# Transposing gated blocks by DMA: the steps of a block set one or more steps apart

## The chip, the cores and the metric

The kernel runs on one core of one Trainium2 chip. A core has five engines that run their own instruction streams and meet through semaphores: PE (TensorE, matrix products), DVE (VectorE), ACT (ScalarE), POOL (GpSimd) and SP (SyncE, which here only issues DMAs). The metric is the device time of one execution in microseconds (us), the median of several runs. Lower is better.

## The reference

One decoder layer for 256 tokens of width 2048, in float32: half an FFN, a parallel mixer of sliding-window attention and an RWKV-7 recurrence, cross-attention into a memory, half an FFN, and a last norm. The change lies in the two FFNs (inner width 5632):

```python
def swiglu(h, w_gate, w_up, w_down):
    return (jax.nn.silu(h @ w_gate) * (h @ w_up)) @ w_down
...
        x = x + 0.5 * swiglu(rms_norm(x, ffn1_norm[l]), ffn1_w_gate[l], ffn1_w_up[l], ffn1_w_down[l])
        x = gated_parallel_mixer(x, mix_norm[l], ...)
        x = memory_cross_attention(x, mem, cross_norm[l], ...)
        x = x + 0.5 * swiglu(rms_norm(x, ffn2_norm[l]), ffn2_w_gate[l], ffn2_w_up[l], ffn2_w_down[l])
    return rms_norm(x, final_norm)
```

## The kernel before

**Products.** A float32 factor is split into a high part, rounded to the type that TensorE multiplies (fp32r), and the rest. A product is then three: high by high, rest by high, high by rest (`times`, L449, L450, L451). Weights stream from HBM in pieces of 1 MB (`raw`, L326). ACT casts the high part `hi` (L372), DVE subtracts for the rest `lo` (L373). PE's matmuls add up in PSUM banks named `acc`, `mm` and `tr`.

**Gate and up together.** `gate_and_up` works out a block of 512 inner columns of both weights through `product_pair`: eight steps q over the width of 2048, two chunks of 128 rows each. Some steps (q = 0, 2, 4 in the first FFN, 0, 2, 3, 4 in the second) are done as seven products instead of eight, by a scheme like Strassen's: DVE forms four combinations of the gate and up weights (L401 to L404), ACT casts them (`thi`, L380), DVE subtracts (`tlo`, L381). For q = 3 the combinations were staged in DRAM (`sums`) and are loaded from there. After the last of the seven-product steps ACT copies a PSUM bank into the new block `hb` (L593), and DVE adds up the results (L596 to L608) into the gated block: `hb`, 256 tokens by 512 columns, as [128, 2, 512].

**Turning a block.** The down product needs the gated block with its columns on the partitions. An FFN has 11 blocks in three groups of 4, 4 and 3. The last block of each group is transposed by TensorE, the other eight, sixteen in both FFNs, by DMA: the generator `turned`. Its transposes work on 16-bit elements, so a float32 block goes as two halves. ACT copies the low and the high halves of all words apart (two `uh`, L761), four DMA transposes on SP's queue bring them into `ht` (L767; the first two carry the one half, the other two the other half), four ACT copies join the halves to float32 words again (two for each of two tiles `u`, L772: the first needs transposes one and two, the second three and four), and each `u` is split (`hhi` by ACT, L649, `hlo` by DVE, L650).

**What sets the order.** `turned` runs in the background of the next block's `gate_and_up`: `Interleave.tick` resumes each running generator up to its next `yield`, and `product_pair` ticks three times in a seven-product step, four times in another one. So a `yield` is one step, a dozen matmuls or less. Where the last seven-product step ends, `first` runs all steps that are still left (`until`), since it needs the tiles. From the start of `gate_and_up` to there are 15 ticks in the first FFN, 14 in the second. Each engine works through its own instructions in the order that results, ACT's and SP's included; the tile scheduler may move PE's.

Blocks are numbered 0 to 15 here, in the order in which they are turned: 0 to 7 in the first FFN, 8 to 15 in the second. Block 7 is turned from 618 us on, block 12 from 1876 us on.

Of the kernel before, what the change touches and what calls it, by code (L numbers as in the profile page):

```python
# [137 lines left out]
def decoder_layer(ctx: ExitStack, tc: tile.TileContext, a: dict, out: bass.AP):  # L138
    nc = tc.nc
    act, dve, pool, pe = nc.scalar, nc.vector, nc.gpsimd, nc.tensor  # L140
# [18 lines left out]
    def f32(x):  # L159
        return x.bitcast(F32)  # L160
# [14 lines left out]
    def idle(n):  # L175
        for _ in range(n):
            yield
# [94 lines left out]
    for entry in weight_plan(a):  # L272
# [10 lines left out]
        for k in range(k0, k0 + nk, 2 * KU):  # L283
            u = len(units)
# [294 lines left out]
    def sums_of(sp):  # L579
        return (sp.tile([P, 512], F32, tag="u", name="u", bufs=2) for _ in range(2))  # L580
# [56 lines left out]
    def feat(tok, cols):  # L637


        b = tr()  # L640
        for i, col in enumerate(cols):
            for t in range(2):
                o = (2 * i + t) * P
                pe.transpose(b[:, o : o + P], tok[:, t, col : col + P], ident[:])  # L644
        return b[:].rearrange("p (c t) -> p c t", c=2)

    def split(x: Act, c, n, src):

        act.copy(x.at(0, c, n), src)  # L649
        dve.tensor_tensor(x.at(1, c, n), src, f32(x.at(0, c, n)), ALU.subtract)  # L650
        x.done |= set(range(c, c + n))
# [81 lines left out]
    def feed_forward(sp, x, norm: Norm, wg, wu, wd, done, begin_last=lambda: None, last=False):  # L733
        if last:
            for tag, shape, dt, bufs in (
                ("hhi", [P, 16, T], F32R, 1), ("hlo", [P, 16, T], F32R, 1),
                ("hb", [P, 2, 512], F32, 2), ("thia", [P, KU, 512], F32R, 1),
                ("tloa", [P, KU, 512], F32R, 1), ("thib", [P, KU, 512], F32R, 1),
                ("tlob", [P, KU, 512], F32R, 1),
            ):  # L740
                sp.tile(shape, dt, tag=tag, name=tag, bufs=bufs)
        begun = at["item"]
        c = combinations(
            sp, norm.x, SEVEN_2 if last else SEVEN, "c",
            lambda: at["item"] > begun + (4 if last else 7) and not (last and norm.r is None),
        )
        c["next"] = []
        for gi, (j0, nj) in enumerate(GROUPS):
            h = Act(
                [sp.tile([P, 16, T], F32R, tag="hhi", name="hhi")],  # L750
                [sp.tile([P, 16, T], F32R, tag="hlo", name="hlo")], 16,
            )
            ch = combinations(sp, h, SEVEN_DOWN[nj < 4], "d", early=False, n=12)

            def turned(hb, c):

                both = hb[:].rearrange("p t n -> p (t n)")
                src = both.bitcast(U16).rearrange("p (t n e) -> p e t n", t=2, e=2)
                us = [sp.tile([P, 2, 512], U16, tag="u", name="uh", bufs=2) for _ in range(2)]
                for e, u in enumerate(us):  # L760
                    act.copy(u[:], src[:, e])  # L761
                    yield
                dst = sp.tile([P, 2, 2, 4, P], U16, tag="hb", name="ht", bufs=2)
                yield
                for e, u in enumerate(us):
                    for t in range(2):
                        nc.sync.dma_start(dst[:, e, t], u[:, t], transpose=True)  # L767
                yield from idle(7)
                for q, u in enumerate(sums_of(sp)):
                    v = u[:].bitcast(U16).rearrange("p (c t k e) -> p e t c k", c=2, t=2, e=2)  # L770
                    for e in range(2):
                        act.copy(v[:, e], dst[:, e, :, 2 * q : 2 * q + 2, :])  # L772
                    split(h, c + 2 * q, 2, u[:].rearrange("p (c t) -> p c t", c=2))
                    yield

            def transposed(hb, c):
                banks = [feat(hb, [2 * q * P, (2 * q + 1) * P]) for q in range(2)]
                for q, b in enumerate(banks):
                    split(h, c + 2 * q, 2, b)
                    yield  # L780

            for j in range(j0, j0 + nj):
                if j > 0:
                    hb = gate_and_up(sp, norm.x, c, norm.r, wg)

                    turn = transposed if j == j0 + nj - 1 else turned
                    c["next"].append(turn(hb, 4 * (j - j0)))
                    continue
                pg = product(norm.x, wg)
                hb = sp.tile([P, 2, 512], F32, tag="hb", name="hb", bufs=2)  # L790
                if last:
                    for t in range(2):
                        act.activation(hb[:, t, :], pg[t][:], AF.Silu, scale=norm.r[t])
                pu = product(norm.x, wu, bank=acc if last else mm)
                bg.until(lambda: norm.r is not None)
                for t in range(2):
                    if not last:
                        act.activation(hb[:, t, :], pg[t][:], AF.Silu, scale=norm.r[t])
                    dve.scalar_tensor_tensor(
                        hb[:, t, :], pu[t][:], norm.r[t], hb[:, t, :], ALU.mult, ALU.mult  # L800
                    )
                c["next"].append(turned(hb, 0))
            end = gi == len(GROUPS) - 1
            bg.spawn("feat", c["next"].pop())
            if end:
                begin_last()

            def col(t, n):
                return x[:, t, n * 512 : (n + 1) * 512]

            for n in (0, 2):
                if last and end and n:

                    whole = [(t, slice(0, 512)) for t in range(2)]
                    parts_ = [(t, slice(c, c + 256)) for t in range(2) for c in (0, 256)]
                    pieces = {2: whole, 3: parts_}
                    for m in (n, n + 1):
                        pd = product(h, wd, skew=m == 3)
                        for t, cs in pieces[m]:
                            dve.scalar_tensor_tensor(  # L820
                                col(t, m)[:, cs], pd[t][:, cs], 0.5, col(t, m)[:, cs],
                                ALU.mult, ALU.add,
                            )
                            done(m, t, cs)
                    continue
                down(h, ch, wd, [[col(t, n + i) for i in range(2)] for t in range(2)])
                if end:
                    done(n)
                    done(n + 1)
# [1018 lines left out]
```

## Time and profile before

| | |
|---|---|
| median of 3 runs | 2250.27 us (2247.72 to 2253.74) |
| the profiled execution | 2251.8 us |
| its span, first to last instruction | 2250.1 us |
| mean granted clock of TensorE | 0.998 |
| PE busy | 2205.8 us, 98% of the span |
| DVE busy | 1800.1 us, 80% |
| ACT busy | 1341.4 us, 60% |
| DMA transposes | 64, median 5.0 us from issue to landing |

Durations in the trace are of one instruction on its engine; a bracket such as [4.50 <-DMA ht<-uh] tells how long the engine had been idle before it and what ended that. Matmuls overlap: in a row without waits they start 0.23 us apart, and are shown 0.39 us long. SPq is the DMA-issuing work of SP. A line of the view by stages has the stage's bounds, its length, and for each engine the busy time with the number of instructions in brackets.

### The profile page before, as it was taken

To read this page: it belongs to the slowest core of one execution; us is meant where nothing else is said; L and a number is where in the kernel's file an instruction comes from. 1 tells how busy PE (TensorE), PEld (TensorE's weight loads), DVE (VectorE), ACT (ScalarE), POOL (GpSimd) and SP (SyncE) were. 2 spreads that over 40 slices of the span, in tenths; PEclk is the share of its full clock that TensorE was granted. 3 is DMA by queue.
4 is the path that set the end of the run, shared out by engine and by line. 5 is a ranking of instruction groups with operands and counts; after the bars stand their busy time and mean duration, and the time that the engine had idled before them with its cause. 6 is when DMAs were issued, how large, how long until landed. Compare 5 with 4: busy or idle time off the path is not lost.

```text
span 2250.1 us, 28118 instructions
## 1 busy us (share of the span) xinstructions
PE 2205.8 (98%) x10392; PEld 1803.5 (80%) x10392; DVE 1800.1 (80%) x2316; ACT 1341.4 (60%) x1773; POOL 107.0 (5%) x184
## 2 busy tenths in 40 slices
PE   9999999999999999999999999999999999999998
PEld 7778877788878877888888888888768877788776
DVE  7888888898989476877667666458898898998896
ACT  6665556664666577644544546466665566655664
POOL 0000000000000001000331030000000000000000
PEclk9999999999999999999999999999999999999999
DMA  8665666656575645677778787557766666666673
GB/s 301 188 214 187 205 199 213 197 192 220 196 196 194 190 127 161 206 233 213 227 219 282 217 282 252 185 169 274 219 204 217 209 211 213 221 208 204 204 248 135
DMA packets 233097, 474.41 MB, mean 211 GB/s; under 512 B 50336, under 2 KB 52736, under 8 KB 221952
## 3 DMA queue, kind: packets, MB, share of 16 engines
q1 hardware_dynamic: 223792, 446.48, 61.2%
q0 software_dynamic: 7648, 23.52, 3.4%
q10 hardware_dynamic: 1520, 2.63, 0.3%
q8 instruction: 81, 1.33, 0.2%
q14 instruction: 56, 0.46, 0.1%
HBM read 440.49 MB, written 23.59 MB: 206 GB/s over the span
## 4 chain that ended last, share of the span: by engine, by line
PE 76%; DVE 12%; DMA 6%; ACT 2%; issue 2%; SPq 1%; POOLq 0%; POOL 0%; ACTq 0%; DVEq 0%
PE acc L449 17%; PE acc L450 17%; PE acc L451 17%; PE mm L449 5%; PE mm L451 5%; PE mm L450 5%; DVE lo L373 4%; DMA raw<-in_ffn_w_up_dram 3%; DVE tlo L381 2%; DMA ht<-uh 1%; PE tr L644 1%; PE tr L450 1%; PE tr L451 1%; PE tr L449 1%; PE mm L1468 1%
## 5 line engine op out<-in xcount | busy, mean ns | idle before, releaser
L373 DVE TENSOR_TENSOR lo<-raw,hi 128x1024 fp32r<-128x1024 f32 (+1 forms) x768 | 878.3, 1149 | 342.2 <-ACT hi L372 339.7
L372 ACT CAST hi<-raw 128x1024 fp32r<-128x1024 f32 (+1 forms) x768 | 754.4, 992 | 659.4 <-PE acc L451 482.9
L450 PE MATMUL acc<-lo,xhi 128*128 128x512 f32 (+1 forms) x1134 | 441.1, 389 | 8.5 <-DVE lo L373 8.3
L449 PE MATMUL acc<-hi,xhi 128*128 128x512 f32 (+1 forms) x1134 | 444.0, 394 | 5.1 <-ACT hi L372 4.7
L451 PE MATMUL acc<-hi,xlo 128*128 128x512 f32 (+1 forms) x1134 | 439.3, 388 | 0.0
L450 PEld LDWEIGHTS acc<-lo,xhi 128*128 128x128 f32 x1134 | 213.5, 188 | 56.3 <-DVE lo L373 14.9
L449 PEld LDWEIGHTS acc<-hi,xhi 128*128 128x128 f32 x1134 | 213.3, 188 | 53.4 <-ACT hi L372 7.7
L451 PEld LDWEIGHTS acc<-hi,xlo 128*128 128x128 f32 x1134 | 212.9, 188 | 43.1 <-issue 0.4
L381 DVE TENSOR_TENSOR tlo<-raw,thi 128x1024 fp32r<-128x1024 f32 x192 | 232.0, 1219 | 5.2 <-ACT thi L380 4.5
L380 ACT CAST thi<-raw 128x1024 fp32r<-128x1024 f32 x192 | 199.5, 1050 | 49.9 <-DVE raw L403 30.6
L449 PE MATMUL mm<-hi,xhi 128*128 128x512 f32 x402 | 157.3, 392 | 1.5 <-DVE u L598 1.2
L450 PE MATMUL mm<-lo,xhi 128*128 128x512 f32 x402 | 157.0, 391 | 0.0
L451 PE MATMUL mm<-hi,xlo 128*128 128x512 f32 x402 | 156.9, 390 | 0.0
L451 PE MATMUL acc<-hi,hlo 128*128 128x512 f32 x372 | 145.3, 391 | 0.0
L450 PE MATMUL acc<-lo,hhi 128*128 128x512 f32 x372 | 145.3, 391 | 0.0
L449 PE MATMUL acc<-hi,hhi 128*128 128x512 f32 x372 | 145.0, 390 | 0.0
L449 PEld LDWEIGHTS mm<-hi,xhi 128*128 128x128 f32 x402 | 75.7, 188 | 19.7 <-DVE u L598 3.9
L451 PEld LDWEIGHTS mm<-hi,xlo 128*128 128x128 f32 x402 | 75.8, 188 | 16.0
L450 PEld LDWEIGHTS mm<-lo,xhi 128*128 128x128 f32 x402 | 75.7, 188 | 15.6
L450 PEld LDWEIGHTS acc<-lo,hhi 128*128 128x128 f32 x372 | 69.9, 188 | 14.3
L449 PEld LDWEIGHTS acc<-hi,hhi 128*128 128x128 f32 x372 | 69.9, 188 | 14.2
L451 PEld LDWEIGHTS acc<-hi,hlo 128*128 128x128 f32 x372 | 69.9, 188 | 14.1
(445 smaller groups left out, 3583.4 us busy)
## 6 DMA issues: line engine op xcount, KB each, us to landing
raw<-in_ffn_w_down_dram SPq DMA_DIRECT2D x88, 1024.0 KB, 5.2
raw<-in_ffn_w_gate_dram SPq DMA_DIRECT2D x84, 1024.0 KB, 5.3
raw<-in_ffn_w_up_dram SPq DMA_DIRECT2D x78, 1024.0 KB, 6.2
raw<-in_w_in_dram SPq DMA_DIRECT2D x136, 512.0 KB, 3.9
raw<-in_w_out_dram SPq DMA_DIRECT2D x32, 512.0 KB, 4.7
raw<-sums SPq DMA_DIRECT2D x20, 512.0 KB, 6.8
raw<-in_w_proj_attn_dram SPq DMA_DIRECT2D x16, 512.0 KB, 3.9
raw<-in_w_proj_rwkv_dram SPq DMA_DIRECT2D x16, 512.0 KB, 6.4
```

Of the source, the lines that this page charges most:

```text
L372: at["hi"] = act.copy(hi[:, s], raw[:, s])
L373: at["lo"] = dve.tensor_tensor(lo[:, s], raw[:, s], f32(hi[:, s]), ALU.subtract)
L380: act.copy(hi[:], v[:])
L381: dve.tensor_tensor(lo[:], v[:], f32(hi[:]), ALU.subtract)
L449: pe.matmul(o, xh, hi, start=first, stop=False, **how)
L450: pe.matmul(o, xh, lo, start=False, stop=False, **how)
L451: pe.matmul(o, xl, hi, start=False, stop=last, **how)
L644: pe.transpose(b[:, o : o + P], tok[:, t, col : col + P], ident[:])
L1468: pe.matmul(vb[to, (o + k) * P : (o + k + 1) * P][:, r], lhs(k, e), v[:, k, r], start=v is u and k + e == 0, stop=True, **ek,)
```

## The change

Only the generator `turned` is edited. The two copies `uh` come one step later than before and with idle steps between them; every DMA transpose is a step of its own; there are two idle steps before the joins rather than seven; and the joins and the split of each half are two steps.

```diff
--- before.py
+++ after.py
@@ -757,19 +757,21 @@
                 both = hb[:].rearrange("p t n -> p (t n)")
                 src = both.bitcast(U16).rearrange("p (t n e) -> p e t n", t=2, e=2)
                 us = [sp.tile([P, 2, 512], U16, tag="u", name="uh", bufs=2) for _ in range(2)]
-                for e, u in enumerate(us):
-                    act.copy(u[:], src[:, e])
-                    yield
+                yield
+                act.copy(us[0][:], src[:, 0])
+                yield from idle(3)
+                act.copy(us[1][:], src[:, 1])
                 dst = sp.tile([P, 2, 2, 4, P], U16, tag="hb", name="ht", bufs=2)
-                yield
                 for e, u in enumerate(us):
                     for t in range(2):
                         nc.sync.dma_start(dst[:, e, t], u[:, t], transpose=True)
-                yield from idle(7)
+                        yield
+                yield from idle(2)
                 for q, u in enumerate(sums_of(sp)):
                     v = u[:].bitcast(U16).rearrange("p (c t k e) -> p e t c k", c=2, t=2, e=2)
                     for e in range(2):
                         act.copy(v[:, e], dst[:, e, :, 2 * q : 2 * q + 2, :])
+                    yield
                     split(h, c + 2 * q, 2, u[:].rearrange("p (c t) -> p c t", c=2))
                     yield
```

The steps of a block were 13 and are 15. Before: copy; copy; (the tile); four DMAs and seven idle steps; joins and split; joins and split. Now: nothing; copy and three idle; copy, the tile and the first DMA; three DMAs, one a step; two idle; joins; split; joins; split. From the tile on, lines stand two further down (L772 becomes L773), and the second copy is L763. Every engine has the same instructions as before, and as many of them; what changes is where they stand. Three places:

SyncE, block 7. `raw` are the weight loads, `ht<-uh` the transposes. Before:

```order
L326 DMA raw_4918<-in_ffn_w_gate_dram 128x2048
L326 DMA raw_4974<-in_ffn_w_up_dram 128x2048
L767 DMA_TRANSPOSE ht<-uh 128x4x128
L326 DMA raw_5017<-in_ffn_w_gate_dram 128x2048
L767 DMA_TRANSPOSE ht<-uh 128x4x128 x3
L326 DMA raw_5069<-in_ffn_w_up_dram 128x2048
```

Now:

```order
L326 DMA raw_4918<-in_ffn_w_gate_dram 128x2048
L326 DMA raw_4974<-in_ffn_w_up_dram 128x2048
L767 DMA_TRANSPOSE ht<-uh 128x4x128
L326 DMA raw_5015<-in_ffn_w_gate_dram 128x2048
L767 DMA_TRANSPOSE ht<-uh 128x4x128 x2
L326 DMA raw_5068<-in_ffn_w_up_dram 128x2048
L767 DMA_TRANSPOSE ht<-uh 128x4x128
```

The second up load from the top stood behind all four transposes and now stands ahead of the fourth. It is so in each of the sixteen blocks, with gate loads standing between or ahead of the earlier transposes; in blocks 9 and 12 the gate load and the staged sums now also stand ahead of the first.

ACT, block 7, from the cast of the next step's `thi` on; `u<-ht` are the joins. Before:

```order
L380 CAST thi<-raw 128x1024
L372 CAST hi<-raw_4974 128x512
L380 CAST thi<-raw 128x1024
L772 COPY u<-ht 128x2x2x128 x2
L372 CAST hi<-raw_4918 128x1024
L649 CAST hhi<-u 128x512
L772 COPY u<-ht 128x2x2x128 x2
L372 CAST hi<-raw_4974 128x1024
L372 CAST hi<-raw_5017 128x1024
L649 CAST hhi<-u 128x512
L380 CAST thi<-raw 128x1024
L372 CAST hi<-raw_5069 128x512
```

Now:

```order
L380 CAST thi<-raw 128x1024
L372 CAST hi<-raw_4974 128x512
L380 CAST thi<-raw 128x1024
L773 COPY u<-ht 128x2x2x128
L372 CAST hi<-raw_4918 128x1024
L372 CAST hi<-raw_4974 128x1024
L372 CAST hi<-raw_5015 128x1024
L380 CAST thi<-raw 128x1024
L773 COPY u<-ht 128x2x2x128
L380 CAST thi<-raw 128x1024
L649 CAST hhi<-u 128x512
L372 CAST hi<-raw_5068 128x512
```

Ahead of the cast of raw_4918's second half stands one join rather than two, and the other three, with both `hhi`, went behind the next casts `hi`; the second stands between the two `thi`, the last two behind them. Blocks 3, 4 and 6 read the same. In blocks 0, 1, 2 and 5 the new order is join, hi, hi, join, join, hhi, join, thi, hi, hhi, thi. In the second FFN (blocks 9, 10, 12, 13, 15 alike) it was join, thi, join, join, hhi, join, hi of the up load, hhi, hi of the gate, the copy of L593, thi, thi; it is join, thi, join, join, hi of the up load, hhi, thi, join, thi, hi, hi, hhi, the copy.

TensorE, block 12, the start of the last seven-product step; hi_15686 is the gate load's first half, hi_15690 the up load's, hi_15738 before the gate load's second half, thi_15682 and thi_15694 the combinations. Before:

```order
L449 MATMUL mm_15557<-hi_15686,xhi_12481 128x512
L450 MATMUL mm_15557<-lo_15687,xhi_12481 128x512
L451 MATMUL mm_15557<-hi_15686,xlo_12482 128x512
L449 MATMUL acc_15561<-hi_15686,xhi_12481 128x512
L450 MATMUL acc_15561<-lo_15687,xhi_12481 128x512
L451 MATMUL acc_15561<-hi_15686,xlo_12482 128x512
L449 MATMUL mm_15566<-hi_15690,chi_12745 128x512
L449 MATMUL acc_15561<-hi_15738,xhi_12481 128x512
L450 MATMUL mm_15566<-lo_15691,chi_12745 128x512
L451 MATMUL mm_15566<-hi_15690,clo_12746 128x512
L449 MATMUL tr_15546<-thi_15682,chi_12745 128x512
L449 MATMUL tr_15550<-thi_15682,chi_12745 128x512
```

Now:

```order
L449 MATMUL mm_15556<-hi_15686,xhi_12481 128x512
L450 MATMUL mm_15556<-lo_15687,xhi_12481 128x512
L451 MATMUL mm_15556<-hi_15686,xlo_12482 128x512
L449 MATMUL tr_15546<-thi_15682,chi_12745 128x512
L449 MATMUL tr_15550<-thi_15682,chi_12745 128x512
L449 MATMUL acc_15560<-hi_15686,xhi_12481 128x512
L450 MATMUL acc_15560<-lo_15687,xhi_12481 128x512
L451 MATMUL acc_15560<-hi_15686,xlo_12482 128x512
L449 MATMUL mm_15565<-hi_15690,chi_12745 128x512
L450 MATMUL mm_15565<-lo_15691,chi_12745 128x512
L451 MATMUL mm_15565<-hi_15690,clo_12746 128x512
L449 MATMUL acc_15569<-thi_15694,xhi_12481 128x512
```

The two matmuls on thi_15682 stood behind ten others of this step and now stand behind three; the second half of the gate weights no longer comes ahead of them. On DVE, the `lo` of that second half stood behind L481, three small operations of the next combinations (L487 to L489), an `hlo` (L650) and another small one (L490), and now stands right behind L481.

## The prediction

> **What bounds the kernel now.** I read the busy shares first, then the chain of waits, then the busy time by stage, and last the timelines of two blocks. On the page:
>
> ```profile
> PE 2205.8 (98%) x10392; PEld 1803.5 (80%) x10392; DVE 1800.1 (80%) x2316; ACT 1341.4 (60%) x1773; POOL 107.0 (5%) x184
> ...
> PE 76%; DVE 12%; DMA 6%; ACT 2%; issue 2%; SPq 1%; POOLq 0%; POOL 0%; ACTq 0%; DVEq 0%
> ```
>
> TensorE is busy for 98% of the span and carries 76% of the chain. The change neither adds nor removes a matmul, so it can only shorten or lengthen TensorE's waits. Where these lie shows in the view that cuts the span into stages (length, then busy time and count of PE, PEld, DVE, ACT, POOL, then granted clock, DMA share, GB/s):
>
> ```profile
> 50.00:200.00 150.00, 144.10 (x617) 116.40 (x617) 129.93 (x170) 97.51 (x118) 1.66 (x3) 0.98 0.62 198
> 200.00:310.00 110.00, 110.00 (x486) 90.83 (x485) 96.83 (x113) 60.33 (x67) 0.00 (x0) 1.00 0.57 196
> 310.00:460.00 150.00, 146.28 (x638) 117.86 (x636) 131.60 (x168) 97.82 (x118) 0.00 (x0) 1.00 0.63 205
> ...
> 570.00:660.00 90.00, 86.39 (x375) 69.72 (x374) 75.27 (x94) 57.24 (x68) 0.00 (x0) 1.00 0.68 206
> ...
> 1560.00:1700.00 140.00, 133.82 (x570) 105.15 (x570) 124.36 (x154) 92.44 (x110) 0.00 (x0) 1.00 0.67 216
> ...
> 1820.00:1970.00 150.00, 142.85 (x617) 113.45 (x616) 134.40 (x170) 100.45 (x121) 0.00 (x0) 1.00 0.67 216
> ...
> 2080.00:2180.00 100.00, 96.46 (x418) 76.65 (x417) 88.69 (x110) 68.22 (x84) 2.17 (x4) 1.00 0.70 226
> ```
>
> The six gate-and-up stages, in which the transposes run, leave PE idle for 5.90 + 3.72 + 3.61 + 6.18 + 7.15 + 3.54 = 30.1 us; the down stage between the first two, 200 to 310, leaves none. So this is what there is to win, and any wait made longer here is a loss. DVE is 84 to 90% busy in these stages, close behind, but not full.
>
> What the waits hang on, in block 7 (the eighth of the sixteen blocks that are turned by DMA), by the timelines of SyncE, ACT and PE:
>
> ```profile
> 619.29 1.19 SPq L767 DMA_TRANSPOSE ht<-uh  x1
> 620.58 0.54 SPq L326 DMA_DIRECT2D raw<-in_ffn_w_gate_dram  x1
> 621.17 5.48 SPq L767 DMA_TRANSPOSE ht<-uh  x3
> 626.75 0.52 SPq L326 DMA_DIRECT2D raw<-in_ffn_w_up_dram  x1
> ```
>
> ```profile
> 629.58 0.77 ACT L772 COPY u<-ht 128x512 uint16<-128x512 uint16 x1 [4.50 <-DMA ht<-uh]
> 630.51 0.76 ACT L772 COPY u<-ht 128x512 uint16<-128x512 uint16 x1 [0.16 <-DMA ht<-uh]
> 631.14 1.03 ACT L372 CAST hi<-raw 128x1024 fp32r<-128x1024 f32 x1
> ...
> 637.01 1.06 ACT L380 CAST thi<-raw 128x1024 fp32r<-128x1024 f32 x1 [0.65 <-DVE raw L403]
> ```
>
> ```profile
> 632.23 0.51 PE L449 MATMUL acc<-hi,xhi 128*128 128x512 f32 x1 [1.58 <-ACT hi L372]
> 633.48 0.50 PE L450 MATMUL acc<-lo,xhi 128*128 128x512 f32 x1 [0.75 <-DVE lo L373]
> ...
> 639.90 0.50 PE L450 MATMUL tr<-tlo,chi 128*128 128x512 f32 x1 [0.44 <-DVE tlo L381]
> ```
>
> Two things are late. ACT works in order, so its cast `hi` of the gate weights stands behind two joins that wait for transposes, and PE waits 1.58 us for that cast. And the next up load is issued at 626.75, 0.10 after the last transpose's issue ends (621.17 + 5.48): it is queued behind it on SyncE.
>
> **The change part by part.** The counts of copies, DMAs, joins and splits stay the same, so no engine does more work. What moves is order.
>
> *The up load goes ahead of the fourth transpose.* The price of an issue, over all 64, and the time to landing:
>
> ```profile
> L767 SPq DMA_TRANSPOSE ht<-uh x64: 1188/1281/2969, 59.9 to 2143.4; - x64
> ...
> DMA to landing us min/median/max: 2.4/5.0/8.3
> ```
>
> If issue sets the load's time, the load gains one issue: 1.28 us at the median, 5.48/3 = 1.83 in block 7. If the rings set it, it gains only the bytes of one transpose ahead of it. In block 7 the second pair landed by 630.51, the first by 629.58, so about 0.93/2 = 0.46 for each. I take the middle of 0.46 and 1.46 (block 12, below), 0.96: the queue shows room for the one in some blocks and not in others. The fourth transpose in turn lands behind a 1 MB load instead of ahead of it, about 0.46 after the load's landing (the spacing again). [...]
>
> *Blocks 3, 4, 6 and 7: three of four joins go behind the casts.* One join, which needs the first pair of transposes only, now stands ahead of `hi` in place of two: `hi` can start at 629.58 + 0.63 = 630.21 rather than at 631.14 (0.63 is the distance from 630.51 to 631.14). PE gets 0.93 of its 1.58 back. What is late next is the lo for the same weights (0.75), which moves along with `hi`. Bounds for a block: 0 (the cast then waits for something else) to 0.93 + 0.44 (the wait for tlo goes too) = 1.37. I take 0.93 for each: 4 x 0.93 = **3.7**.
>
> *Blocks 0, 1, 2 and 5.* There the second join, which needs the fourth transpose, stays ahead of `thi`. From its landing follow two joins, an `hhi` and a join (0.63 + 0.63 + 0.53 + 0.63), so `thi` starts about 0.46 + 2.42 = 2.9 us after the up load's landing. What the combinations on DVE would allow is read in block 12:
>
> ```profile
> 1892.77 0.69 DVE L401 TENSOR_TENSOR raw<-raw,raw 128x512 f32<-128x512 f32 x1 [0.93 <-DMA raw<-in_ffn_w_up_dram]
> ...
> 1893.98 0.68 DVE L403 TENSOR_TENSOR raw<-raw,raw 128x512 f32<-128x512 f32 x1
> ...
> 1900.07 2.35 DVE L373 TENSOR_TENSOR lo<-raw,hi 128x1024 fp32r<-128x1024 f32 x2
> ```
>
> They end 1893.98 + 0.68 - 1892.77 = 1.9 after the landing. So 1.0 is given back of a load that is 0.46 to 1.83 sooner: -0.5 to +0.8, the middle of it rounded to 0.3 (the up load, not `thi`, is what PE's wait leads to there): 4 x 0.3 = **1.2**.
>
> *Second FFN, blocks 9, 10, 12, 13 and 15.* The waits and the queues of block 12 (SyncE, ACT and PE):
>
> ```profile
> 1879.79 4.39 SPq L767 DMA_TRANSPOSE ht<-uh  x3
> 1884.29 0.53 SPq L326 DMA_DIRECT2D raw<-in_ffn_w_up_dram  x1
> ```
>
> ```profile
> 1893.35 0.61 ACT L649 CAST hhi<-u 128x512 fp32r<-128x512 f32 x1
> ...
> 1895.29 1.99 ACT L380 CAST thi<-raw 128x1024 fp32r<-128x1024 f32 x2
> ```
>
> ```profile
> 1893.49 0.50 PE L449 MATMUL mm<-hi,chi 128*128 128x512 f32 x1 [0.17 <-ACT hi L372]
> 1894.96 0.50 PE L449 MATMUL acc<-hi,xhi 128*128 128x512 f32 x1 [0.96 <-ACT hi L372]
> ...
> 1896.39 0.73 PE L449 MATMUL tr<-thi,chi 128*128 128x512 f32 x2 [0.34 <-ACT thi L380]
> 1897.34 0.50 PE L449 MATMUL acc<-thi,xhi 128*128 128x512 f32 x1 [0.21 <-ACT thi L380]
> ...
> 1901.34 0.50 PE L450 MATMUL acc<-lo,xhi 128*128 128x512 f32 x1 [0.99 <-DVE lo L373]
> ```
>
> The shown waits add up to 2.67. The last is for a `lo` that DVE starts 1900.07 - 1892.77 = 7.3 after the load lands. In the new order the two `thi` lie apart (a join between), the first from 0.46 + 2 joins + hi + hhi, about 2.8 after the landing against 1895.29 - 1892.77 = 2.5; but that `lo` loses five small DVE operations ahead of it (1.4 us by the starts from 1898.66 on), so it starts 6.7 to 7.3 after the landing: 0 to 0.6 gained. With the load's 0.96 that is 0.96 + 0.3 = 1.26 in each, 5 x 1.26 = **6.3** (bounds 0.46 to 2.67 each). Blocks 8, 11 and 14, where the load matters less, I give half of 0.96, three times: **1.5** (bounds 0 to 1.46 each).
>
> *The tail.* In the second FFN the steps just about fill their ticks, and the last split's `hhi` (0.61) and the two gate casts come ahead of the copy that frees PSUM for the next sums. Hidden while DVE is not yet there; bounds 0 to 0.61 in eight blocks, half of it: **-2.4**. The spreading of the two copies `uh` I set at nothing: they keep their 1.05 each, and ACT idles 4.50 us before the first join.
>
> Sum: 3.7 + 1.2 + 6.3 + 1.5 - 2.4 = 10.3. The profiled execution took 2251.8 (span 2250.1 and 1.7 around it), so 2241.5; the median of the runs is 1.5 lower than that execution, so **2240** for the median. With every bound at its good end the gain is 4 x 1.37 + 4 x 0.8 + 5 x 2.67 + 3 x 1.46 = 26.4; with every one at its bad end -2.0 + 2.3 - 4.9 = -4.6, a loss: 2224 to 2255.
>
> **The rivals.** *1. Slower: the fourth transpose is the new wait.* If the up load does not get sooner (it is served by the rings at the same time), everything that ACT has behind the second join is late: 1.0 in each of blocks 0, 1, 2 and 5, and up to 0.46 + 2 x 0.63 = 1.7 in the eight blocks of the second FFN, where the cast of the up weights stands behind it too, 4.0 + 13.6 = 17.6, less the 3.7 of blocks 3, 4, 6, 7: +13.9, **2264**. For it speaks that ACT runs in order and that the shown landing takes up to 8.3 us. Against it: the load was queued 0.10 behind an issue. It decides from the point at which the transpose lands over 1.9 us minus two joins after the load, about 0.6.
>
> *2. Nothing to tell.* The load is ring-bound (0.46, not 0.96) and ACT gives it back in the second FFN: 3.7 + 5 x 0.46 - 2.4 = 3.6, **2247**. For it: in block 7 the two later transposes landed right behind the first. Against: DMA share is only 0.62 to 0.70 in these stages.
>
> *3. The clock.* Two waits of this trace were long enough to cost clock after them. One, and what followed it:
>
> ```profile
> 76.00:79.00 3.00, 1.21 (x3) 0.80 (x4) 3.00 (x5) 2.83 (x4) 0.00 (x0) 0.93 0.22 90
> 79.00:82.50 3.50, 3.50 (x11) 2.71 (x11) 3.32 (x4) 0.72 (x2) 0.00 (x0) 0.58 0.00 0
> ```
>
> PE was busy 1.21 of 3 us, then ran at 0.58 for 3.5 us, which costs 3.5 x 0.42 = 1.5. In the second FFN's new order only three matmuls of the last seven-product step precede the ones on `thi`; before, it was ten. So the four waits of block 12 run together into one of up to 2.7 us. If that trips the clock in all five such blocks, 5 x 1.5 = 7.5 is lost: 10.3 - 7.5 = 2.8 gained, **2247**. Against it: the clock stays 1.00 in the second FFN's stages, though these have 3.5 to 7.2 us of idle in pieces. [...]
>
> **How the numbers follow.** Less than 0.3% (6.8 us) can't be told from no change here. Forecast, 2240 and thereabouts: 0.55, faster. Rival 1: 0.25, slower. Rival 2: 0.15 and rival 3: 0.05, both the same. So faster 0.55, same 0.20, slower 0.25. The forecast's own range is 2230 to 2247 (gains of 3 to 20; all good ends at once are unlikely). The range for 8 in 10 is **2230 to 2262**: about 0.07 lies below it, and 0.12 above, the upper half of rival 1.
>
> **What would show it.** Right: PE's idle time in the six stages falls from 30.1 to about 20; the up load starts within 0.1 of the third transpose's issue end and lands 0.5 to 1.5 sooner; in block 7 the wait of 1.58 for `hi` is near 0.65. Rival 1 shows as ACT's idle before the second join, ended by the transposes, growing from 0.16 to over 1, with `hi` or `thi` behind it and PE waiting for them. Rival 2: loads land as before. Rival 3: stretches of granted clock near 0.55 in the second FFN. Wrong altogether would be a loss in the down stages, where nothing is idle now and only the lateness of the last split could reach.

## The result, and the profile after

The changed kernel takes 2228.84 us, median of 4 runs (2225.44 to 2231.03), beside 2249.23 for the kernel before on the same chip: a ratio of 0.9905, 95% interval 0.9885 to 0.9924. A second set of runs gave 2225.63 beside 2244.86, ratio 0.9913 (0.9898 to 0.9928). So the time falls by about 20 us, twice the 10.3 of the sum, and the median lies 1.2 us below the range. The profiled execution of the changed kernel took 2231.0, span 2229.3.

From the page, the busy shares and the chain that ended last:

```profile
PE 2196.5 (99%) x10392; PEld 1801.8 (81%) x10392; DVE 1800.3 (81%) x2316; ACT 1340.0 (60%) x1773; POOL 106.8 (5%) x184
...
PE 74%; DVE 14%; DMA 7%; ACT 3%; issue 2%; SPq 0%; DVEq 0%; POOLq 0%; POOL 0%; ACTq 0%
```

The counts are those of before. SyncE's queue has gone from 1% to 0% of the chain. The six gate-and-up stages, by the view of stages (the same columns as in the prediction):

```profile
50.00:200.00 150.00, 147.89 (x646) 119.30 (x645) 136.43 (x175) 100.19 (x121) 0.00 (x0) 1.00 0.61 199
...
310.00:460.00 150.00, 147.32 (x642) 118.46 (x641) 132.85 (x169) 97.54 (x117) 0.00 (x0) 1.00 0.63 206
...
570.00:660.00 90.00, 88.39 (x391) 71.88 (x390) 77.60 (x99) 58.61 (x72) 0.00 (x0) 1.00 0.70 218
...
1560.00:1700.00 140.00, 136.25 (x594) 109.49 (x593) 128.24 (x162) 95.58 (x117) 0.00 (x0) 1.00 0.67 218
...
1820.00:1970.00 150.00, 144.61 (x632) 116.59 (x631) 138.20 (x174) 100.49 (x121) 0.00 (x0) 1.00 0.68 223
...
2080.00:2180.00 100.00, 95.88 (x416) 76.02 (x415) 89.22 (x112) 65.81 (x81) 2.17 (x4) 1.00 0.70 231
```

PE's idle time is 2.11 + 2.68 + 1.61 + 3.75 + 5.39 + 4.12 = 19.7, where 30.1 stood and "about 20" was foretold. Yet the span fell by 20.8. Shown idle time counts too little: a matmul is shown 0.39 us long though the next can start 0.23 after it, so each wait is 0.16 longer than shown, and time at half clock counts as busy (from 79.00 to 82.50 us of the first profile, at a granted clock of 0.58, all 3.50 us). By the starts of matmuls (what lies between two starts beyond 0.23), the waits of the sixteen blocks add up to 48.3 us before and 30.9 after. The granted clock of the first stage is 1.00 now and was 0.98: its two stretches at half clock are gone.

Block 7, by the timelines of SyncE, ACT and PE:

```profile
610.59 3.19 SPq L767 DMA_TRANSPOSE ht<-uh  x2
613.88 0.52 SPq L326 DMA_DIRECT2D raw<-in_ffn_w_up_dram  x1
614.45 1.19 SPq L767 DMA_TRANSPOSE ht<-uh  x1
```

```profile
617.92 0.77 ACT L773 COPY u<-ht 128x512 uint16<-128x512 uint16 x1 [3.35 <-DMA ht<-uh]
618.56 2.94 ACT L372 CAST hi<-raw 128x1024 fp32r<-128x1024 f32 x3
623.96 1.04 ACT L380 CAST thi<-raw 128x1024 fp32r<-128x1024 f32 x1 [2.47 <-DVE raw L403]
624.91 0.78 ACT L773 COPY u<-ht 128x512 uint16<-128x512 uint16 x1
```

```profile
620.91 0.50 PE L450 MATMUL acc<-lo,xhi 128*128 128x512 f32 x1 [0.29 <-DVE lo L373]
...
625.12 0.50 PE L450 MATMUL mm<-lo,chi 128*128 128x512 f32 x1 [1.20 <-DVE lo L373]
```

The load is issued 0.10 after the third transpose's issue ends (613.88, after 610.59 + 3.19 = 613.78), as foretold. The three casts follow the first join at once, and PE's wait of 1.58 for `hi` is gone. What is late next is a `lo`, 0.29 and 1.20.

Block 12, ACT and PE:

```profile
1871.81 1.41 ACT L773 COPY u<-ht 128x512 uint16<-128x512 uint16 x2 [2.13 <-DMA ht<-uh]
...
1874.13 1.04 ACT L380 CAST thi<-raw 128x1024 fp32r<-128x1024 f32 x1
```

```profile
1875.22 0.73 PE L449 MATMUL tr<-thi,chi 128*128 128x512 f32 x2 [1.25 <-ACT thi L380]
```

Here ACT does wait 2.13 us for the fourth transpose, as the first rival has it, and PE 1.25 for the `thi` behind it.

### The profile page after: what moved, and what is told of

It is laid out like the page before. It is cut to its first block, busy times and chain, and to the rows that moved or that the text cites. A ratio compares the mean times of both kernels' runs of the same rounds, so it can differ in the third digit from the quotient of the medians.

```text
span 2229.3 us, 28131 instructions
## 1 busy us (share of the span) xinstructions
PE 2196.5 (99%) x10392; PEld 1801.8 (81%) x10392; DVE 1800.3 (81%) x2316; ACT 1340.0 (60%) x1773; POOL 106.8 (5%) x184
## 4 chain that ended last, share of the span: by engine, by line
PE 74%; DVE 14%; DMA 7%; ACT 3%; issue 2%; SPq 0%; DVEq 0%; POOLq 0%; POOL 0%; ACTq 0%
PE acc L449 16%; PE acc L450 16%; PE acc L451 16%; DVE lo L373 5%; PE mm L450 5%; PE mm L451 5%; PE mm L449 5%; DMA raw<-in_ffn_w_up_dram 3%; DVE tlo L381 3%; DMA ht<-uh 3%; PE tr L644 1%; PE mm L1470 1%; PE tr L450 1%; PE tr L449 1%; ACT hi L372 1%
## 5 line engine op out<-in xcount | busy, mean ns | idle before, releaser
L401 DVE TENSOR_TENSOR raw<-raw,raw 128x512 f32<-128x512 f32 x86 | 59.3, 690 | 30.7 <-DMA raw<-in_ffn_w_up_dram 26.3
```

The costliest lines, as they stand in the source:

```text
L401: dve.tensor_tensor(t[1][:, 0], ru[:, 0], rg[:, 0], ALU.subtract)
```

## Which stages gained

A single profile is a poor measure of a stage: three profiles with the order of before (the first, a second one, and the run with the copies alone apart, which takes the same time) have spans of 2250.1, 2244.9 and 2240.6 us. So the table takes the mean of these three, and of three with the new order (the changed kernel twice, and the run in which only the fourth transpose is late). It is made from the starts of matmuls with fixed numbers that lie between the stages: how much sooner the stage is over with the new order, its own part alone, as far as the start of the last matmul.

```
stage                      gained, us   by the prediction's terms
start, up to matmul 60        0.7          0
blocks 0 to 2                 4.1          3 x 0.3            = 0.9
blocks 3 to 5                 2.1          2 x 0.93 + 0.3     = 2.2
blocks 6 and 7                3.0          2 x 0.93           = 1.9
mixer and cross-attention    -0.2          0
blocks 8 to 10                4.6          0.5 + 2 x 1.26     = 3.0
blocks 11 to 13               3.3          0.5 + 2 x 1.26     = 3.0
blocks 14, 15 and the end     1.1          0.5 + 1.26         = 1.8
the tail, over 8 to 15         -           -2.4
together                     18.7          10.3
```

The first rows are the least certain. Blocks 0 to 2 took 213.1, 211.3 and 207.1 us in the three profiles with the order of before (from matmul 60 to matmul 950, in the down stage), and 206.4 to 206.5 in the three with the new one: the gain there lies anywhere from 0.6 to 6.7, and about 1 of the mean of 4.1 is the half clock of a single profile (an estimate from that profile's two stretches of 3.4 us at half clock: 1.7 each, twice, over three profiles). Nothing of the change acts ahead of matmul 60, so the 0.7 there is chance.

By kind of block, from the same six profiles: the 150 matmuls that the next table counts are 1.14 us shorter in each of blocks 0, 1, 2 and 5, 1.12 in 3, 4, 6 and 7, 0.50 in 8, 11 and 14, 0.76 in 10, 13 and 15, and 2.34 in 9 and 12.

And the queue and the load in a block, mean of the sixteen, in us from a matmul of fixed number just ahead of the first copy; the last column is the time of the 150 matmuls from there on:

```
                          up load   up load   fourth transpose   150
                          issued    landed    landed             matmuls
before, second profile    9.11      15.48     11.90              36.91
changed, first profile    7.37      14.22     14.69              36.05
changed, second profile   7.24      13.96     14.41              35.77
only T4 late              7.31      14.00     14.48              35.68
T4 with T3                9.13      15.19     11.72              36.51
joins apart               9.08      15.13     11.69              36.34
a fifth ahead             9.12      15.41     16.11              37.27
joins first               7.32      14.01     14.48              36.30
two behind                5.74      13.27     14.23              35.50
all behind                4.07      12.42     14.42              35.54
```

In the three rows of the new order (the changed kernel twice, only T4 late) the load is issued 1.74 to 1.87 sooner and lands 1.26 to 1.52 sooner. There the fourth transpose lands 0.45 to 0.48 behind it: the forecast's 0.46.

## The experiments

T1 to T4 are the four transposes. "Order of before" and "new order" mean the order on ACT and SyncE.

**The kernel before, once more.**

> The kernel before, once more, for a second profile. Of the 20.8 us between the two profiled spans, 1.9 arise in the first 17 us, ahead of any transpose and with the same order on every engine, and about 3 in two stretches at half clock in blocks 0 and 2. If both belong to the kernel, they come again: the 50th matmul starts near 17.2 us (15.4 in the changed kernel) and two stretches near 0.55 follow the waits of blocks 0 and 2. If they are chance, the start lies anywhere between 15 and 17.5 and the stretches may be missing, with a span of about 2245 to 2250.

2246.59 in one run, span 2244.9; no stretch at half clock in blocks 0 to 2, and the 60th matmul starts 1.4 us sooner than in the first profile (the changed kernel: 1.9). So the two stretches at half clock and the late start are chance, and 5 of the 20.8 us between the first two spans belong to the one execution that was profiled; the medians (2249.23, and 2246.45 in this set of runs) differ less.

**Only T4 late.** In the kernel before:

```diff
                     for t in range(2):
+                        if e and t:
+                            yield from idle(4)
                         nc.sync.dma_start(dst[:, e, t], u[:, t], transpose=True)
-                yield from idle(7)
+                yield from idle(3)
```

> The kernel before with one thing changed: the fourth transpose is issued four steps after the first three. SyncE's order is then that of the changed kernel (up load ahead of the fourth transpose), and the scheduler gives ACT nearly the changed order too, while the two copies, the first three transposes and the joint joins and split stay as before. Theory that the fourth transpose alone makes the gain: 2226 to 2234. Theory that the spreading of copies and joins brings some of it: 2235 to 2245. No gain (2250) would put all of it on the spreading.

2226.21, ratio 0.9909 (0.9891 to 0.9928). One DMA four steps later makes the whole gain. With it, the orders on ACT and SyncE follow: in all sixteen blocks the up load goes ahead of T4, and in blocks 9 and 12 the gate load and the staged sums go ahead of T1, as in the changed kernel.

**T4 with T3.** In the changed kernel:

```diff
                         nc.sync.dma_start(dst[:, e, t], u[:, t], transpose=True)
-                        yield
-                yield from idle(2)
+                        if (e, t) != (1, 0):
+                            yield
+                yield from idle(3)
```

> The changed kernel with one thing undone: the fourth transpose is issued in the step of the third, ahead of the up load. ACT's order falls back to that of before with it; copies, steps of the DMAs and of the joins stay spread. Theory that the fourth transpose alone makes the gain: 2245 to 2254, as before. Theory that the spreading counts: 2232 to 2243.

2240.50, ratio 0.9970 (0.9957 to 0.9982): 14 of the 20 us are gone, 6 stay. By the number this is the second theory's range, yet most of the gain left with T4. SyncE's order is that of before except in blocks 9 and 12, where the gate load and the sums still go ahead of T1; what stays is taken up below.

**The order of the casts alone.** As the last, and three joins are held behind the last weight cast:

```diff
                     for e in range(2):
-                        act.copy(v[:, e], dst[:, e, :, 2 * q : 2 * q + 2, :])
+                        if q == 0 and e:
+                            last_hi = at["hi"].ins
+                        if q or e:
+                            with tc.issue_after(last_hi):
+                                act.copy(v[:, e], dst[:, e, :, 2 * q : 2 * q + 2, :])
+                        else:
+                            act.copy(v[:, e], dst[:, e, :, 2 * q : 2 * q + 2, :])
```

> As the run with the fourth transpose in the step of the third, but three of the four joins are held behind the last weight cast that was written ahead of them, so ACT takes casts first as in the changed kernel, while the up load still stands behind all four transposes. Theory that ACT's order makes most of the gain: 2230 to 2238. Theory that the earlier up load makes most of it: 2242 to 2250. The prediction's terms give ACT's part as 3.7 for blocks 3, 4, 6, 7 and 0 to 0.6 in the second FFN: some 5, so 2245.

2240.47, ratio 0.9973 (0.9962 to 0.9984): the same as without the hold, and between the two ranges. With the up load late, ACT's new order is worth nothing, 2240.5 and 2240.5 (the gate load also passes T1 in blocks 4 and 7 here, which it does not in the run beside it). The prediction's 3.7 for blocks 3, 4, 6 and 7 falls with it.

**Joins first.** The changed kernel with the joins two steps earlier (`idle(0)` for `idle(2)`), and every cast written after them held behind the last join:

```diff
-            at["hi"] = act.copy(hi[:, s], raw[:, s])
+            if at.get("join") is None:
+                at["hi"] = act.copy(hi[:, s], raw[:, s])
+            else:
+                with tc.issue_after(at["join"].ins):
+                    at["hi"] = act.copy(hi[:, s], raw[:, s])
```

(and likewise for `thi`).

> The changed kernel with its joins two steps earlier and the casts written after them held behind the second join, the one that needs the fourth transpose. SyncE's order stays that of the changed kernel in most blocks, but ACT now waits for the fourth transpose ahead of the third cast of weights and both combinations. It prices the prediction's first rival. If ACT in order is what the late transpose strikes, the wait before the second join grows to 2 us or more and the time rises by 0.5 to 1.5 in each of 16 blocks: 2237 to 2252. If PE has enough casts in hand, 2227 to 2233, as the changed kernel.

2237.37, ratio 0.9961 (0.9947 to 0.9975). By the view of one tile, what ACT's joins wait for in the changed kernel:

```profile
L773 ACT COPY u<-ht x64: 750/774/789, 65.7 to 2132.9; 128x512 uint16<-128x512 uint16 x64
its engine sat idle before it (us, times) until:
  DMA ht<-uh: 25.8, 18
```

and with the joins first:

```profile
L781 ACT COPY u<-ht x64: 748/776/789, 66.3 to 2139.8; 128x512 uint16<-128x512 uint16 x64
its engine sat idle before it (us, times) until:
  DMA ht<-uh: 40.4, 31
```

The load lands as soon as in the changed kernel (14.01), but ACT now waits 40.4 us in 31 places, and about half of the gain is lost: 9.6 us beside the next run (2227.82). By blocks, that loss is not spread over all sixteen. Over blocks 0 to 7 the 150 matmuls add up to 281.2 us in both runs, though ACT waits longer there too; all of the loss stands in the second FFN, 8.5 us. Of these, 3.5 are in blocks 9 and 12, where the gate load and the sums have fallen back behind T1, a second change beside the intended one. The other five, mostly 0.8 to 1.7 in each of blocks 10, 11, 13 and 15, have SyncE's order unchanged. So the first rival's mechanism is real in the second FFN, at some 5 us here, and the order that the scheduler gave ACT in the changed kernel avoids it.

**Joins held in the changed kernel.** The hold from above, on the changed kernel.

> The changed kernel with three of four joins held behind the last weight cast that was written ahead of them; SyncE's order is unchanged. Theory that all of the gain is the load's landing and none of it ACT's order: 2225 to 2232, no different. Theory that the late fourth transpose costs something (ACT waits 0.58 us a block before the second join): up to 16 x 0.58 = 9 less, 2220.

2227.82, ratio 0.9922 (0.9907 to 0.9937), no different from the changed kernel. What ACT still waits for T4 costs nothing that can be told.

**Two behind, and all behind.** T3 with T4, or all four, in the step of T4:

```diff
+                        if (e, t) == (1, 0):
+                            yield
                         nc.sync.dma_start(dst[:, e, t], u[:, t], transpose=True)
-                        yield
+                        if (e, t) != (1, 0):
+                            yield
```

```diff
+                        if (e, t) == (0, 0):
+                            yield from idle(3)
                         nc.sync.dma_start(dst[:, e, t], u[:, t], transpose=True)
-                        yield
-                yield from idle(2)
+                yield from idle(3)
```

> The changed kernel with the third transpose behind the up load as well: two transposes go ahead of it and two behind. Theory that each us of earlier landing is a us of the time: the load is issued 1.3 earlier again and lands 0.5 (bytes of one transpose) to 1.3 sooner, 16 x 0.5 to 16 x 1.3 = 8 to 20 less than the changed kernel, 2209 to 2221. Theory that the wait is gone from most blocks by now: 2224 to 2229. Theory that the late pair now holds ACT: over 2231.

> The changed kernel with all four transposes in the step of the fourth; in most blocks three or four of them then stand behind the up load. Two behind gave 2224.6. Theory that landing still counts: the load another 0.5 to 1.3 sooner, 2208 to 2220. Theory that what is left of the waits has other causes: 2220 to 2226. Theory that the late transposes now bind (the joins come 2 us later and the steps must end by the last seven-product step): 2228 to 2240.

2224.55, ratio 0.9904 (0.9889 to 0.9919), and 2223.76, ratio 0.9903 (0.9888 to 0.9918). The changed kernel in the set of the second: 2225.63, 0.9913. The step from one to four behind is about 2 us and, by the ratios, not clear of noise. Yet the load lands another 0.69 and 1.54 sooner (13.27 and 12.42, for 13.96) and the 150 matmuls are shorter by no more than 0.27: what is left of the waits hangs on something else, and the gain has run out. In the run with all behind, the clock fell after one wait, in the very block of the third rival:

```profile
1868.00:1873.00 5.00, 2.70 (x12) 1.88 (x11) 3.02 (x5) 4.92 (x8) 0.00 (x0) 0.95 1.02 386
1873.00:1876.40 3.40, 3.40 (x11) 2.63 (x10) 3.40 (x7) 3.24 (x6) 0.00 (x0) 0.56 0.03 11
```

The same shows in two runs without the early load: with T4 beside T3 in block 12 (granted clock 0.51 from 1887.5 to 1890.9 us), and with the casts' order alone in block 10 (0.50 from 1674.5 to 1677.9).

**Only the copies apart.** The kernel before, the second copy three steps later:

```diff
-                for e, u in enumerate(us):
-                    act.copy(u[:], src[:, e])
-                    yield
-                dst = sp.tile([P, 2, 2, 4, P], U16, tag="hb", name="ht", bufs=2)
                 yield
+                act.copy(us[0][:], src[:, 0])
+                yield from idle(3)
+                act.copy(us[1][:], src[:, 1])
+                dst = sp.tile([P, 2, 2, 4, P], U16, tag="hb", name="ht", bufs=2)
...
-                yield from idle(7)
+                yield from idle(6)
```

> The kernel before with the second copy three steps later and nothing else spread; SyncE's order is that of before in every block. The run with the fourth transpose back in the step of the third gained 0.3%, and its PE time over a block is shorter by some 2 us in blocks 9 and 12, the two in which the gate load and the staged sums go ahead of the first transpose there. If that order made the 0.3%, this run shows none of it: 2244 to 2249. If the spread copies made it, 2239 to 2243.

2246.00, ratio 1.0002 (0.9993 to 1.0011). The copies are worth nothing, as the prediction set them.

**Only joins and split apart.** The kernel before with the one `yield` between the joins and the split. It was run for the 6 us that stayed in the run with T4 beside T3.

> The kernel before with joins and split of each half in two steps and nothing else. In the first FFN both queues keep the order of before; in blocks 9 and 12 SyncE issues the gate load and the two staged sums ahead of the first transpose, as in the changed kernel, and the up load stays behind all four. If that order makes the 0.3% that stays when the fourth transpose goes back to the third: 2238 to 2242, all of it in the second FFN. If not: 2243 to 2248.

2238.73, ratio 0.9974 (0.9963 to 0.9985). The first FFN keeps its order; in block 9, and likewise in block 12, SyncE now issues the gate load and the sums ahead of T1:

```profile
1607.83 0.37 SPq L326 DMA_DIRECT2D raw<-in_ffn_w_gate_dram  x1
1608.25 0.97 SPq L343 DMA_DIRECT2D raw<-sums  x2
1609.26 6.30 SPq L767 DMA_TRANSPOSE ht<-uh  x4
1615.66 0.53 SPq L326 DMA_DIRECT2D raw<-in_ffn_w_up_dram  x1
```

This and the run with T4 beside T3 have that order in blocks 9 and 12 in common and gain the same 0.3%, 6 to 7 us; the copies alone, without it, gain none. The 150 matmuls of block 9 take 36.1 instead of 38.2 in the second profile of before, those of block 12 37.6 instead of 39.7. So 4.2 us stand in the two blocks. The rest of the second FFN's 6.8 stands in blocks where SyncE keeps its order: 0.7, 0.8, 0.4 and 1.0 in blocks 8, 10, 13 and 15. There other orders changed with the edit: on DVE an `hlo` goes later in all eight blocks, in blocks 9, 10, 12, 13 and 15 behind a `lo` of the weights, and ACT's order changes in blocks 9, 12 and 15. That this shortens those blocks is likely, not shown, and its share in blocks 9 and 12 is not separated either.

**The changed kernel again, and a fifth transpose ahead.** T3 once more, into a tile that nobody reads, ahead of the up load:

```diff
+                more = sp.tile([P, 4, P], U16, tag="more", name="more", bufs=1)
...
                         nc.sync.dma_start(dst[:, e, t], u[:, t], transpose=True)
+                        if e and not t:
+                            nc.sync.dma_start(more[:], u[:, t], transpose=True)
                         yield
```

> The changed kernel once more, beside the next two on the same chip: a ratio near 0.9905 to the kernel before, and a second profile: PE's waits in the blocks about as in the first (30 us by the starts of matmuls, 48 in the first profile of before).

> The changed kernel with a fifth transpose (the third once more, into a tile that nobody reads) ahead of the up load; the real fourth stays behind it, and ACT's order is in the main that of the changed kernel. The up load is then issued and lands about as late as before the change, while everything else is as after. Theory that the landing of the up load makes the gain, one for one: the gain is gone, 2243 to 2250. Theory that the order of the casts makes it: no different from the changed kernel, 2226 to 2232.

2249.33, ratio 1.0025 (1.0009 to 1.0041): one more transpose on SyncE ahead of the load, its issue and its bytes, and the gain is gone, and more. Block 0 in three kernels, by the timeline of all engines: SyncE's issue of the load, the first DVE operation on it, the cast `thi` that follows, and PE's waits. Before (second profile):

```profile
64.93 0.52 SPq L326 DMA_DIRECT2D raw<-in_ffn_w_up_dram  x1
...
72.71 0.69 DVE L401 TENSOR_TENSOR raw<-raw,raw 128x512 f32<-128x512 f32 x1 [2.31 <-DMA raw<-in_ffn_w_up_dram]
...
74.64 1.05 ACT L380 CAST thi<-raw 128x1024 fp32r<-128x1024 f32 x1 [2.07 <-DVE raw L403]
...
75.73 0.50 PE L449 MATMUL tr<-thi,chi 128*128 128x512 f32 x1 [1.58 <-ACT thi L380]
...
77.53 0.50 PE L450 MATMUL tr<-tlo,chi 128*128 128x512 f32 x1 [1.29 <-DVE tlo L381]
```

Changed (first profile), with the second join besides:

```profile
62.70 0.51 SPq L326 DMA_DIRECT2D raw<-in_ffn_w_up_dram  x1
...
68.67 0.69 DVE L401 TENSOR_TENSOR raw<-raw,raw 128x512 f32<-128x512 f32 x1
...
69.12 1.42 ACT L773 COPY u<-ht 128x512 uint16<-128x512 uint16 x2 [0.81 <-DMA ht<-uh]
...
71.55 1.04 ACT L380 CAST thi<-raw 128x1024 fp32r<-128x1024 f32 x1
...
73.91 0.50 PE L450 MATMUL tr<-tlo,chi 128*128 128x512 f32 x1 [0.43 <-DVE tlo L381]
```

With the fifth ahead:

```profile
62.49 1.35 SPq L770 DMA_TRANSPOSE more<-uh  x1
63.94 0.52 SPq L326 DMA_DIRECT2D raw<-in_ffn_w_up_dram  x1
...
71.31 0.70 DVE L401 TENSOR_TENSOR raw<-raw,raw 128x512 f32<-128x512 f32 x1 [2.79 <-DMA raw<-in_ffn_w_up_dram]
...
72.00 1.41 ACT L776 COPY u<-ht 128x512 uint16<-128x512 uint16 x2 [3.78 <-DMA ht<-uh]
...
74.88 0.50 PE L449 MATMUL tr<-thi,chi 128*128 128x512 f32 x1 [1.70 <-ACT thi L380]
```

The fifth transpose costs the load 1.24 at issue (63.94 - 62.70). It makes two things late at once: the load, and behind it T4 with the join, 3.78 of wait. By the table of blocks the load then lands 1.45 later than in the second profile of the changed kernel (15.41 and 13.96), and 150 matmuls take 1.50 longer (37.27 and 35.77): with the orders in the main held, each us by which the load and T4 come later is about a us of the time. (Some 0.2 of the 1.50 is chance: the run with the fifth has two stretches of 3.4 us at half clock, in blocks 0 and 2, the other none.) The other way it does not hold, as the runs with two and all behind show.

## Why the prediction was half right

**The mechanism held.** The up load was queued behind T4 on SyncE, and freeing it shortens PE's waits in the blocks. Place and side effects came as worked out: issue right behind T3 (0.10 in block 7), T4 0.45 to 0.48 behind the load, the wait for `hi` in block 7 gone, the copies worth nothing, the stretches at half clock absent in the second FFN of both its profiles.

**The step that failed is the size and the reach of the load's term.** It was put at 0.96, the middle of 0.46 (the author's estimate for the bytes of one transpose, half of the 0.93 between two joins) and 1.46 (one issue). The load is issued 1.74 to 1.87 sooner, more than the upper bound, and lands 1.26 to 1.52 sooner: of the two candidates, the issue is the nearer one. And it was counted in full in five blocks, by half in three, almost given back in four, and not at all in four. The table of stages has a gain in every group. Against the 18.7 of that table the sum of 10.3 lacks 8.4: 3.4 for blocks 0, 1, 2 and 5, 2.4 for the tail, 0.8 for blocks 3, 4, 6 and 7, 0.7 for the other five of the second FFN, 0.7 of chance ahead of matmul 60, and the rest elsewhere.

- Blocks 0, 1, 2 and 5: 1.0 was to be given back, since `thi` stands behind a join that waits for T4. It is: in block 0 `thi` starts 71.55 - 68.67 = 2.9 after the load's first use, as foretold, instead of 1.9 (74.64 - 72.71 before). But PE no longer waits for it: the load has come so much sooner that the delay falls into slack. So the term was 0.3 a block and measured 1.14 in the mean, the largest miss (2.6 in block 0, which varies most from profile to profile, and 0.7 in each of the others). (The middle of its bounds, -0.5 and +0.8, would have been 0.15; the 0.3 is not what they give.)
- Blocks 3, 4, 6 and 7: about the right number from a wrong cause. 3.7 was credited to ACT taking the cast ahead of the second join; that order alone gives nothing. Nor does it give anything with the load late behind a fifth transpose: the 150 matmuls of these four blocks add up to 147.1 us there, 145.1 in the second profile of before and 138.3 in the second of the changed kernel. The load, with T4 behind it, gives it.
- Second FFN: 6.3 for five blocks and 1.5 for three, 7.8 together, against 9.0 measured over its three groups. That this is near is luck. The five blocks were to gain 1.26 each; blocks 10, 13 and 15 gain 0.76, and blocks 9 and 12 2.34. In these two the gate load and the sums now go ahead of T1, worth some 4 us by two runs. The order showed it ahead of time, and no term was made of it.
- The tail: -2.4 for the last split and the copy of L593. No run shows it; blocks 14 and 15 with the end gain 1.1 in the mean, though 0.1 in the first profile of the changed kernel.

**Rival 1** was priced at +13.9 should the load not come sooner. The run with the fifth transpose is that case: its load is as late as before and T4 behind it. It is slower than the kernel before, by 0.25% or some 5 us, and its time is 9 us above that of the run with T4 beside T3 (2249.3 and 2240.5; by the ratios 0.55%, 12 us), which has the load as late and T4 early. So the price was right in kind; its condition, a load that comes no sooner, did not come about. **Rival 2**, a load that gains only 0.46, falls: it landed 1.26 to 1.52 sooner. That the rings bind a load no run shows; what the runs show is when it is issued and when it lands. **Rival 3** did not come about in the changed kernel; its sign, half clock in the second FFN, shows in three other profiles (all behind, T4 beside T3, the casts' order alone), once in each.

What stays open: a T4 behind a late load costs 9 to 12, and the load 1.45 and T4 1.70 sooner bring some 24 back. Whether T4 behind an early load still costs something is not measured by itself, since no run has the load early and T4 early too. The run with the joins held, in which ACT does not wait for T4 ahead of the joins at all and takes as long as the changed kernel, speaks for a cost of nothing or little. Nor is it separated how the 6 us that stay without the early load divide between the loads that pass T1 in blocks 9 and 12 and the other orders that change in the second FFN.

## What to carry to other kernels

On a queue that issues in order, as SyncE's did here (in block 7 the load's issue began 0.10 us after that of the transposes ahead of it had ended, 626.75 after 626.65 before and 613.88 after 613.78 now), ask of every DMA how long its issue holds up the next one, and which of the two somebody waits for: here four transposes of 1.3 us each at the median stood ahead of a load that TensorE waited for, and the last of them could land 2.8 us later (14.69 for 11.90) at no visible cost. Price such a move by the queue's gap between the two issues, not by the median of the instruction, and count it in every repetition until a run shows slack. And read a list of reordered rows to its end: about a fifth of this gain, some 4 us, lay in two blocks in which loads pass the first transpose, away from the place that the terms were made for. The same holds for an experiment: two edits here changed an order beside the intended one, and only the times of the single blocks tell how much may have come from it.

## What the runs showed of the hardware

Idle time shown for PE understates its waits, by 0.16 us each here (0.39 shown for a matmul, 0.23 from start to start), and a stretch at half clock counts as busy (3.50 of 3.50 us at 0.58, in block 0 of the first profile of before). Two profiles of the kernel before differed by 5.2 us in span: 1.4 up to the 60th matmul, ahead of any transpose, and 1.8 in blocks 0 to 2, where the first has two stretches of 3.4 us at half clock and the second, with waits as long in block 0 (1.58 and 1.29, for 1.35 and 1.29), has none. Nine such stretches stand between 60 and 2190 us in the fourteen profiles. In the 3.4 us ahead of each, TensorE is shown busy for 0.8 to 2.2 us: 0.8 and 1.2 ahead of the two in the first profile of before. A transpose's issue took from 1.19 to 3.67 us on SyncE in the changed kernel, 1.30 at the median: so what a load gains by passing one can vary from place to place.
